# A decoder trunk on one Trainium2 core: token-major router logits, a larger ring of expert weights, whole rows to DRAM

## The chip, the core and the metric

The kernel runs on one NeuronCore of a Trainium2 chip. Its five engines run their own instruction streams in order: TensorE (PE; its weight loads are listed as PEld), VectorE (DVE), ScalarE (ACT), GpSimd (POOL) and SyncE (SP), which here only issues DMAs. What orders one engine after another are semaphores. The metric is the device time of one execution in microseconds, as the median of some runs.

## The reference, cut to what matters

Two layers, each a mixer, a cross-attention into 256 memory tokens and a mixture of experts; 256 tokens of width 1024, 16 experts of width 512.

```python
for layer in range(DEPTH):                         # DEPTH = 2
    xn = rms_norm(h, norm_mix[layer])
    h = h + (even_mixer(xn, ...) if layer % 2 == 0 else short_conv_mixer(xn, ...))
    h = h + memory_cross_attn(rms_norm(h, norm_xattn[layer]), mem, norm_mem[layer], ...)
    h = h + hier_moe(rms_norm(h, norm_ffn[layer]), ...)
return rms_norm(h, norm_final)

def hier_moe(xn, w_group, b_group, w_expert, b_expert, w_gate, w_up, w_down):
    g_prob = softmax(xt @ w_group + b_group)       # 4 groups
    g_top, g_idx = top_k(g_prob, 1)
    e_logits = (xt @ w_expert + b_expert).reshape(n, 4, 4)
    e_top, e_idx = top_k(e_logits[arange(n), g_idx[:, 0]], 2)
    w = softmax(e_top) * g_top
    ...
    for e in range(16):
        y = y + gate[:, e:e+1] * ((silu(xt @ w_gate[e]) * (xt @ w_up[e])) @ w_down[e])
```

## The kernel before

Tokens lie in two tiles of 128 (`tt` 0 and 1); the residual `h` stays in SBUF as [128, 2, 1024] in float32. A norm sums squares (`square_sum`, on ScalarE with "S", on VectorE with "V"; the squares themselves go to scratch tiles `junkS`, `junkV`), takes a power on GpSimd (`rstd_of`, L237), scales into `xs`, and TensorE transposes it through PSUM banks `nB`, `nC` (`norm_T`, L255). Projections of the mixers and of cross-attention run in split precision: each weight chunk `w` is cast on ScalarE to `hi` (L282), VectorE subtracts for `lo` (L283), both from a pool `spl` of three buffers a tag, and TensorE multiplies the token halves `xh`, `xl` with them (L324, L327, L329 into `FA`; L303 to L305 into `TA`). Layer 1 also norms and transposes the memory tokens (`mem`, halves `m1h`, `m1l`) at the start of its mixer.

The expert stage (`moe`) begins with the route. TensorE transposes `h` (L801) into banks of the tags B and C (two buffers each), copies make `hTr` (L802). The router then multiplies with its 20 columns `wr` as the stationary side and 256 tokens as the moving side (`lg`, L464), copies the result out (`lgT`, L467 and L468), turns it token-major with a small matmul against `two_id` (`lp`, L472), and VectorE adds the bias and ranks the experts (`lo` L483, `scratch` L488 to L491). The functions `busy` put filler matmuls between (L88). Meanwhile the normed tokens `xs` are made in half precision as a high part (L808, L809) and a low part: `low_part` does tile 0 on VectorE (L812), and tile 1 as a scaling on ScalarE (L816) and a subtraction on GpSimd (L817). `dispatch` builds a selection matrix `Pm` (L568) and gathers the 64 tokens of each expert by matmuls (`gB`, L101), scaled into `XgT` (L590, L592).

Experts go in eight pairs. Their weights come as 98 chunks a layer, most of 1 MB, in a fixed order (gate of pair n, down of pair n-1, up of pair n), each into a slot of `ring`; SyncE (L672) issues the next chunk of a slot once the matmuls that used its last content are done, and keeps at most eight loads under way. The ring takes buffers that are idle in that stage: `extra` (NX of 1 MB), `act8`, `kvp`, the six `w` and the three `hi`/`lo` pairs, so that with NX = 6 it has 20 slots. The results of the first six pairs go back by rows: `y` is scaled from PSUM (L743 on VectorE, L745 on ScalarE), an indirect DMA of GpSimd (L746) writes it to DRAM (`Yd`) in halves of 512 columns, and `get_rows` reads it back at the end; the last two pairs come back through a matmul (`PT`). An `If` handles experts with more than 64 tokens.

What sets the order: the framework's scheduler orders each engine's instructions by the program's dependences; `first()` raises the priority of a block, and `mm` or `keep_in_program_order` pins an instruction to the written order.

## Time and profile before

| | |
|---|---|
| median of 3 runs | 955.02 us (953.09 to 956.59) |
| profiled execution | 953.4 us, span 951.4 us |
| mean granted TensorE clock | 0.978 |
| TensorE busy | 890.1 us, 94% |
| VectorE, ScalarE, GpSimd busy | 396.8, 323.4, 82.1 us |
| moved by DMA | 285.45 MB, 300 GB/s over the span |

An execution's own time is the span from the first to the last instruction and what lies around it, here 2.0 us. A busy share is an average over stages of different kinds, so the views below are read by stage: layer 0's mixer and cross-attention up to about 266 us, its route to 285, its experts to about 500, and the same again for layer 1 with the route at 711 to 729 and the experts to about 933.

### The profile page before, as it was taken

The page shows a single profiled execution, that of the slowest core. Times are in us where ns is not written, and L with a number is a line of the kernel's source. Part 1 is how long each engine was busy: PE and PEld are TensorE (multiplying, and loading weights), DVE is VectorE, ACT ScalarE, POOL GpSimd, SP SyncE. Part 2 cuts the span into 40 slices and gives each one's busy share as a digit, 9 for nine tenths or more (in the row PEclk, how much of TensorE's full clock was granted, in tenths as well). Part 3 has the DMA queues.
Part 4 walks back from the last instruction along what each step waited for, and adds up shares of the span by engine and source line. Part 5 has one row for each costly group of instructions (what it writes and reads, how often), then busy time and mean ns, then how long its engine had stood idle before and what let it go on. Part 6 is the DMA issues. An engine that isn't in the chain of part 4 may idle for free. (4 is left out here: it accounts for less than half of the span.)

```text
span 951.4 us, 13242 instructions
## 1 busy us (share of the span) xinstructions
PE 890.1 (94%) x5205; PEld 582.5 (61%) x5205; DVE 396.8 (42%) x842; ACT 323.4 (34%) x597; POOL 82.1 (9%) x136
## 2 busy tenths in 40 slices
PE   7999999999989998899789999999998999899975
PEld 5898779898853333533238998998874333343322
DVE  5846587644452111112057655644444111112106
ACT  4545584654421111011018444635432111111002
POOL 1000060000030001000100000000003000000201
PEclk9989999999999999899999999999999999999998
DMA  7856156657969999999996556558886999999993
GB/s 255 289 185 141 28 172 206 190 202 297 364 226 404 418 420 419 415 421 418 412 385 208 183 182 199 151 174 301 319 315 244 422 417 421 415 420 418 415 407 126
DMA packets 83024, 285.45 MB, mean 300 GB/s; under 512 B 15113, under 2 KB 16225, under 8 KB 62469
## 3 DMA queue, kind: packets, MB, share of 16 engines
q1 hardware_dynamic: 78468, 272.82, 76.3%
q0 software_dynamic: 4480, 11.65, 3.3%
q8 instruction: 45, 0.74, 0.3%
q14 instruction: 31, 0.25, 0.1%
HBM read 275.94 MB, written 11.53 MB: 302 GB/s over the span
## 5 line engine op out<-in xcount | busy, mean ns | idle before, releaser
L283 DVE TENSOR_TENSOR lo<-w,hi 128x1024 fp32r<-128x1024 f32 x122 | 147.7, 1222 | 124.2 <-ACT hi L282 84.3
L282 ACT CAST hi<-w 128x1024 fp32r<-128x1024 f32 x122 | 125.9, 1046 | 87.7 <-PE FA L329 48.0
L101 PE MATMUL egA<-we,XgT 128*64 128x512 f32 x512 | 122.3, 613 | 10.4 <-DVEq L825 6.4
L101 PE MATMUL euA<-we,XgT 128*64 128x512 f32 x512 | 116.8, 593 | 6.3 <-DMA we<-in_moe_w_up_dram 6.3
L101 PEld LDWEIGHTS euA<-we,XgT 128*64 128x64 f32 x512 | 40.0, 137 | 79.1 <-issue 62.0
L101 PE MATMUL eyA<-we,hT 128*64 128x512 f32 x256 | 74.5, 609 | 9.7 <-DMA we<-in_moe_w_down_dram 6.7
L101 PEld LDWEIGHTS egA<-we,XgT 128*64 128x64 f32 x512 | 37.8, 140 | 72.7 <-issue 58.4
L101 PE MATMUL eyO<-we,hT 128*64 128x512 f32 x256 | 73.7, 607 | 0.0
L327 PE MATMUL FA<-xh,hi 128*128 128x256 f32 x272 | 70.4, 292 | 1.8 <-ACT xh L258 1.6
L329 PE MATMUL FA<-xl,hi 128*128 128x256 f32 x272 | 69.6, 289 | 1.8 <-DVE xl L259 1.8
L590 ACT ACTIVATE XgT<-gB,ffn 128x128 f32<-128x128 f32 x64 | 21.8, 365 | 132.9 <-DVE XgT L592 132.9
L327 PEld LDWEIGHTS FA<-xh,hi 128*128 128x128 f32 x272 | 53.3, 196 | 3.6 <-ACT xh L258 2.3
L329 PEld LDWEIGHTS FA<-xl,hi 128*128 128x128 f32 x272 | 53.1, 195 | 3.2 <-DVE xl L259 2.6
L101 PEld LDWEIGHTS eyA<-we,hT 128*64 128x64 f32 x256 | 20.2, 140 | 48.9 <-issue 34.7
L746 POOL DMA_INDIRECT yd<-y,row x24 | 23.9, 994 | 292.7 <-ACT y L745 273.9
L726 DVE SCALAR_TENSOR_TENSOR hs<-hs,euA 128x512 f32<-128x512 f32 x16 | 11.0, 687 | 84.2 <-PE euA L101 84.2
L101 PEld LDWEIGHTS eyO<-we,hT 128*64 128x64 f32 x256 | 20.8, 140 | 37.5 <-issue 35.8
L324 PE MATMUL FA<-xh,lo 128*128 128x256 f32 x272 | 41.7, 285 | 0.0
L101 PEld LDWEIGHTS <-xs 128*128 128x128 f16 x512 | 33.0, 146 | 13.6 <-issue 13.6
L724 ACT ACTIVATE hs<-egA 128x512 f32<-128x512 f32 x16 | 9.6, 597 | 90.8 <-PE egA L101 68.6
L237 POOL TENSOR_TENSOR rs<-ms,mhalf 128x2 f32<-128x2 f32 x9 | 6.5, 718 | 366.2 <-DVE ms L235 244.9
L743 DVE TENSOR_SCALAR y<-eyO,gslr 128x512 f32<-128x512 f32 x12 | 9.0, 751 | 69.4 <-PE eyO L101 69.4
(415 smaller groups left out, 1569.5 us busy)
## 6 DMA issues: line engine op xcount, KB each, us to landing
we<-in_moe_w_gate_dram SPq DMA_DIRECT2D x58, 1024.0 KB, 13.9
we<-in_moe_w_down_dram SPq DMA_DIRECT2D x54, 1024.0 KB, 15.5
we<-in_moe_w_up_dram SPq DMA_DIRECT2D x52, 1024.0 KB, 18.0
we<-in_moe_w_up_dram SPq DMA_DIRECT2D x24, 512.0 KB, 11.5
w<-in_odd_w_in_dram SPq DMA_DIRECT2D x12, 1024.0 KB, 11.3
w<-in_even_w_in_dram SPq DMA_DIRECT2D x9, 1024.0 KB, 9.0
w<-in_xa_wk_dram SPq DMA_DIRECT2D x8, 1024.0 KB, 5.8
w<-in_xa_wv_dram SPq DMA_DIRECT2D x8, 1024.0 KB, 5.7
```

What stands on the lines that cost most here:

```text
L101: tc.keep_in_program_order(P.matmul(out, w, src, **how))
L237: G.tensor_tensor(rs, ms, mhalf, op=ALU.pow)
L282: S.copy(hi, t)
L283: V.tensor_sub(lo, t, hi.bitcast(F32))
L324: P.matmul(o, lo[:, fs], xh[:, k, :], start=False, stop=(k == J - 1), skip_group_check=True)
L327: P.matmul(o, hi[:, fs], xh[:, k, :], start=(k == 0 and f % 2 == 0), stop=False, skip_group_check=True)
L329: P.matmul(o, hi[:, fs], xl[:, k, :], start=False, stop=False, skip_group_check=True)
L590: S.activation(Xg[pi][:, j, :], src, AF.Copy, scale=g)
L724: S.activation(hs, acc["g"], AF.Tanh, scale=0.5)
L726: V.scalar_tensor_tensor(hs, hs, 0.5, acc["u"], op0=ALU.mult, op1=ALU.mult)
L743: V.tensor_scalar(y, py[nh], gsl, None, op0=ALU.mult)
L746: G.indirect_dma_start(out=Yd[l][nh], out_offset=bass.IndirectOffsetOnAxis(ap=PT[:, 0:1], axis=0), in_=y, in_offset=None, bounds_check=2 * ...
```

## The change

Six edits. (1) The router takes `hTr` as the stationary side, 128 tokens at a time, and `wr` as the moving side of 20 columns: 16 small matmuls straight into token-major logits `lp`, with no `lgT` and no second product. `lp` holds one bank of tag C throughout. (2) The norm's factor is made per token tile; the low part of tile 0 is pinned before the factor of tile 1, the low part of tile 1 is one instruction of VectorE, pinned behind `Pm`, and the gather's matmuls with it come last. GpSimd's two subtractions go. (3) NX = 7, so the ring has 21 slots. (4) Rows go to DRAM as 1024 columns by one indirect DMA a pair, and come back so. (5) `wr` moves into the expert stage's pool, loaded ahead of it; SyncE now loads the bias `rb` of layer 0 before x. (6) The scratch tiles of the squares share the tags `hi`/`lo` with the splits, or are the PSUM bank that was just added; several small tiles share tags.

```diff
-NX = 6
+NX = 7
...
-    def load_router(l):
-        t = const.tile([128, J, 20], F32, name=f"wr{l}")
+    def load_router(l, mp):
+        t = mp.tile([128, J, 20], F32, name=f"wr{l}", tag="s2", bufs=3)
...
-    def square_sum(src, acc, eng):
-        junk = (sm if eng == "S" else mix).tile([128, 512], BF16, name="junk" + eng, tag="junk" + eng, bufs=1)
+    def square_sum(src, acc, eng, junk=None):
+        if junk is None:
+            junk = spl.tile([128, 512], BF16, name="junk" + eng, tag="hi" if eng == "S" else "lo")
...
-            square_sum(hs, ss[:, half, tt:tt + 1], "S")
+            square_sum(hs, ss[:, half, tt:tt + 1], "S", ps)
...
-        lg_ps = bank("C", "lg")[:, 0:T]
-        lgT = mp.tile([128, T], F32, name="lgT", tag="s2", bufs=3)
-        G.memset(lgT, 0.0)
-        for j in range(0, J, 2):
-            for i in (0, 1):
-                P.matmul(lg_ps[i * 64:i * 64 + 20, :], wr[l][:, j + i, :], hT[j // 4][:, j % 4 + i, :],
-                         start=(j == 0), stop=(j == J - 2))
-        busy(ident, hT[1][:, 3, :], 4)
-        V.tensor_copy(lgT[0:20, :], lg_ps[0:20, :])
-        V.tensor_copy(lgT[64:84, :], lg_ps[64:84, :])
-        between()
-        lp = bank("C", "lp")[:, 0:2 * 20].rearrange("p (t e) -> p t e", t=TT)
-        for tt in range(TT):
-            P.matmul(lp[:, tt, :], lgT[:, tt * 128:(tt + 1) * 128], two_id, start=True, stop=True)
...
+            order = [(tt, part) for tt in range(TT) for part in range(2)]
+            steps = [(j0, order) for j0 in banks]
+            if late:
+                late()
+                steps = [(j0, order[:-1]) for j0 in banks] + [(j0, order[-1:]) for j0 in banks]
...
-            y = mp.tile([128, 512], F32, name="y", bufs=2)
...
-            G.indirect_dma_start(out=Yd[l][nh], out_offset=bass.IndirectOffsetOnAxis(ap=PT[:, 0:1], axis=0), in_=y,
+            if nh == 0:
+                rows_.append(mp.tile([128, D], F32, name="y", bufs=1))
+                S.activation(rows_[0][:, 0:512], py[nh], AF.Copy, scale=gsl)
+                return
+            V.tensor_scalar(rows_[0][:, 512:D], py[nh], gsl, None, op0=ALU.mult)
+            G.indirect_dma_start(out=Yd[l], out_offset=bass.IndirectOffsetOnAxis(ap=PT[:, 0:1], axis=0), in_=rows_[0],
...
+                for tt in range(TT):
+                    rstd_of(ss_of_h[-1], tt, rs)
+                    if tt:
+                        tc.keep_in_program_order(
+                            V.scalar_tensor_tensor(xsl[:, 0, :], h[:, 0, :], rsx[:, 0:1], xsh[:, 0, :],
+                                                   op0=ALU.mult, op1=ALU.subtract))
+                    V.tensor_scalar(rsx[:, tt:tt + 1], rs[:, tt:tt + 1], SCALE, None, op0=ALU.mult)
...
+                lp = bank("C", "lp")[:, 0:2 * 20].rearrange("p (t e) -> p t e", t=TT)
...
+                            P.matmul(lp[:, tt, :], hj[:, jj, tt * 128:(tt + 1) * 128], wr[l][:, j, :],
+                                     start=(j == 0 and tt == 0), stop=(j == J - 1), skip_group_check=True)
+                busy(ident, hT[1][:, 3, :], 6)
...
-                    for c in (slice(0, 512), slice(512, D)):
-                        t = mp.tile([128, 512], F32, name="xt", tag="XgT", bufs=2)
-                        S.activation(t, h[:, 1, c], AF.Copy, scale=rsx[:, 1:2])
-                        G.tensor_sub(xsl[:, 1, c], t, xsh[:, 1, c])
+                    tc.keep_in_program_order(
+                        V.scalar_tensor_tensor(xsl[:, 1, :], h[:, 1, :], rsx[:, 1:2], xsh[:, 1, :],
+                                               op0=ALU.mult, op1=ALU.subtract))
```

Where the scheduler puts this is seen in three places. First TensorE in layer 0's route, from the last transposes of `h` to the fillers behind the logits; before:

```order
L801 MATMUL nB<-ident,h 128x128 x3
L801 MATMUL nC<-ident,h 128x128 x3
L801 MATMUL nB<-ident,h 128x128 x3
L801 MATMUL nC<-ident,h 128x128 x3
L464 MATMUL lgC<-hTr,wr_1874 20x256 x8
L88 MATMUL busyO<-hTr,ident 128x256 x4
L472 MATMUL lpC<-two_id,lgT 128x20 x2
L88 MATMUL busyO<-lgT,ident 128x256 x6
```

and now:

```order
L809 MATMUL nB<-ident,h 128x128 x6
L815 MATMUL lpC<-wr_2564,hTr 128x20 x4
L809 MATMUL nC<-ident,h 128x128 x4
L815 MATMUL lpC<-wr_2564,hTr 128x20 x8
L809 MATMUL nC<-ident,h 128x128 x4
L815 MATMUL lpC<-wr_2564,hTr 128x20 x4
L88 MATMUL busyO<-hTr,ident 128x256 x6
```

The transposes no longer run through: those of bank C come one bank after the other, with the router's matmuls on the copies between them.

Second the start of layer 1's mixer. ScalarE from the scaling of the tokens on, before:

```order
L247 ACTIVATE xs<-h,rs 128x1024
L207 ACTIVATE junkS,ss<-mem_5949 128x512
L282 CAST hi<-w 128x1024
L258 ACTIVATE xh<-nB,mix_5879 128x256
L258 ACTIVATE xh<-nC,mix_5879 128x256
```

and now, down to the first cast of `w`:

```order
L249 ACTIVATE xs<-h,rs 128x1024
L207 ACTIVATE junkS,ss<-mem_5855 128x512
L260 ACTIVATE xh<-nB,mix_5793 128x256
L260 ACTIVATE xh<-nC,mix_5793 128x256
L260 ACTIVATE xh<-nB,mix_5793 128x256 x2
L260 ACTIVATE xh<-nC,mix_5793 128x256 x2
L260 ACTIVATE xh<-nB,mix_5793 128x256
L207 ACTIVATE junkS,ss<-mem_5855 128x512 x2
L260 ACTIVATE xh<-nC,mix_5793 128x256
L207 ACTIVATE junkS,ss<-mem_5855 128x512
L284 CAST hi<-w 128x1024
```

The cast stood behind the second square of `mem` and ahead of the first `xh`; it stands behind all of both. On TensorE at the same place, now (before, 40 projection matmuls `FA` stood between the last transpose of `xs` and the sixteen of `mem`):

```order
L88 MATMUL busyO<-h,ident 128x256 x2
L329 MATMUL FA<-xh,hi 128x256
L257 MATMUL nB<-ident,mem_5855 128x128
L257 MATMUL nC<-ident,mem_5855 128x128
L257 MATMUL nB<-ident,mem_5855 128x128 x4
L257 MATMUL nC<-ident,mem_5855 128x128 x3
L257 MATMUL nB<-ident,mem_5855 128x128 x3
L257 MATMUL nC<-ident,mem_5855 128x128 x4
L331 MATMUL FA<-xl,hi 128x256
```

One projection matmul is left ahead of the memory's transposes.

Third SyncE at layer 0's restart. The loads `we` up to 2634 (before) and 2618 (now) fill the ring for the first time; the later ones wait for expert matmuls. Before:

```order
L672 DMA we_2610<-in_moe_w_gate_dram 128x2048
L672 DMA we_2624<-in_moe_w_up_dram 128x1024
L672 DMA we_2626<-in_moe_w_up_dram 128x1024
L672 DMA we_2628<-in_moe_w_up_dram 128x1024
L672 DMA we_2630<-in_moe_w_up_dram 128x1024
L672 DMA we_2632<-in_moe_w_up_dram 128x1024
L672 DMA we_2634<-in_moe_w_up_dram 128x1024
L672 DMA we_2829<-in_moe_w_gate_dram 128x2048
L672 DMA we_2831<-in_moe_w_gate_dram 128x2048
```

and now:

```order
L659 DMA we_2594<-in_moe_w_gate_dram 128x2048
L659 DMA we_2606<-in_moe_w_up_dram 128x2048
L659 DMA we_2608<-in_moe_w_up_dram 128x1024
L659 DMA we_2610<-in_moe_w_up_dram 128x1024
L659 DMA we_2612<-in_moe_w_up_dram 128x1024
L659 DMA we_2614<-in_moe_w_up_dram 128x1024
L659 DMA we_2616<-in_moe_w_gate_dram 128x1024
L659 DMA we_2809<-in_moe_w_gate_dram 128x2048
L659 DMA we_2811<-in_moe_w_gate_dram 128x2048
L659 DMA we_2618<-in_moe_w_gate_dram 128x1024
```

The last half chunk of the first filling, 2618, stands behind two loads (2809, 2811) that wait for expert matmuls. In layer 1 the whole ring is filled ahead of the first such load.

## Rows read from the trace of the kernel before

**Rows 1.** Busy by stretch: PE, PEld, DVE, ACT, POOL busy, clock, DMA share, GB/s
```profile
280.00:285.00 5.00, 5.00 (x40) 2.38 (x39) 1.35 (x5) 1.36 (x4) 2.22 (x9) 1.00 0.02 5
520.00:530.00 10.00, 10.00 (x85) 10.00 (x85) 5.50 (x5) 3.83 (x6) 0.00 (x0) 1.00 0.63 210
900.00:910.00 10.00, 7.37 (x24) 1.99 (x21) 0.00 (x0) 0.00 (x0) 0.00 (x0) 0.83 1.02 412
```
**Rows 2.** SyncE's timeline (start, us, issues): the restart in layer 0 and layer 1
```profile
284.80 0.80 SPq L672 DMA_DIRECT2D we<-in_moe_w_gate_dram  x2
...
728.85 4.53 SPq L672 DMA_DIRECT2D we<-in_moe_w_gate_dram  x4
```
**Rows 3.** DMA view from 300 to 360 us, in layer 0's expert stage
```profile
DMA packets 4110, 25.16 MB, mean 419 GB/s; under 512 B 575, under 2 KB 575, under 8 KB 1507
```
**Rows 4.** Timeline of TensorE in layer 0's route (start, us, operation, count, idle before)
```profile
267.38 0.60 PE L801 MATMUL nB<-ident,h 128*128 128x128 f32 x3 [0.78 <-DVE h L223]
...
269.04 1.91 PE L464 MATMUL lgC<-hTr,wr 128*20 128x256 f32 x16
...
273.46 0.59 PE L472 MATMUL lpC<-two_id,lgT 128*128 128x20 f32 x4 [0.58 <-DVE lgT L468]
...
278.95 2.24 PE L101 MATMUL gB<-Pm,xs 128*128 128x128 f16 x32 [1.08 <-DVE Pm L568]
281.12 3.65 PE L101 MATMUL egA<-we,XgT 128*64 128x512 f32 x16
```
**Rows 5.** The same of VectorE
```profile
270.48 0.75 DVE L808 TENSOR_SCALAR xs<-h,rsx 128x1024 f16<-128x1024 f32 x1
271.27 1.28 DVE L812 SCALAR_TENSOR_TENSOR xs<-h,rsx,xs 128x1024 f16<-128x1024 f32 x1
...
274.09 0.38 DVE L483 SCALAR_TENSOR_TENSOR lo<-lpC,rs,rb 128x20 f32<-128x20 f32 x2 [0.78 <-PE lpC L472]
274.51 1.23 DVE L488 TENSOR_TENSOR scratch<-lo 128x160 f32<-128x160 f32 x1
275.66 0.31 DVE L490 TENSOR_TENSOR scratch<-lo 128x160 f32<-128x160 f32 x1
...
278.60 0.51 DVE L568 TENSOR_TENSOR Pm<-iota,posm 128x128 f16<-128x128 f32 x2
```
**Rows 6.** The same of ScalarE
```profile
268.36 1.25 ACT L802 COPY hTr<-nC 128x512 f32<-128x512 f32 x2 [0.22 <-PE nC L801]
```
**Rows 7.** The same of GpSimd
```profile
274.40 1.16 POOL L817 TENSOR_TENSOR xs<-xt,xs 128x512 f16<-128x512 f32 x1 [0.83 <-ACT xt L816]
```
**Rows 8.** Timeline of TensorE at the start of layer 1's mixer
```profile
505.35 0.58 PE L327 MATMUL FA<-xh,hi 128*128 128x256 f32 x2
...
511.86 0.67 PE L255 MATMUL nB<-ident,mem 128*128 128x128 f32 x4
...
513.63 0.36 PE L327 MATMUL FA<-xh,hi 128*128 128x256 f32 x1
```
**Rows 9.** The same of ScalarE
```profile
503.65 1.03 ACT L282 CAST hi<-w 128x1024 fp32r<-128x1024 f32 x1
...
507.70 0.66 ACT L207 ACTIVATE junkS<-mem 128x512 bf16<-128x512 f32 x1
...
508.31 1.07 ACT L282 CAST hi<-w 128x1024 fp32r<-128x1024 f32 x1
509.25 0.51 ACT L258 ACTIVATE xh<-nC,mix 128x256 fp32r<-128x256 f32 x1
509.88 1.15 ACT L247 ACTIVATE mem<-mem,rs 128x1024 f32<-128x1024 f32 x1
```
**Rows 10.** Busy by stretch at the program's start, columns as in rows 1
```profile
12.40:13.90 1.50, 0.38 (x1) 0.19 (x1) 1.50 (x3) 0.98 (x4) 0.00 (x0) 1.00 0.63 95
16.00:18.40 2.40, 2.40 (x14) 2.23 (x13) 0.96 (x6) 1.47 (x2) 0.00 (x0) 0.50 1.05 404
```
**Rows 11.** SyncE's timeline at the program's start
```profile
1.63 0.42 SPq L168 DMA_DIRECT2D mix<-in_norm_mix_dram  x1
```

More of the change, by code (lines that the diff above doesn't have):

```diff
@@ L152, in hybrid_trunk_kernel @@
     dram = ctx.enter_context(tc.tile_pool(name="rows_of", bufs=1, space=bass.MemoryType.DRAM))
-    Yd = [[dram.tile([2 * T, 512], F32, name=f"yd{l}{nh}") for nh in range(2)] for l in range(2)]
+    Yd = [dram.tile([2 * T, D], F32, name=f"yd{l}") for l in range(2)]
     def clear_rows():
-        z = mix.tile([128, 512], F32, name="zero", tag="Pu", bufs=2)
+        z = mix.tile([128, D], F32, name="zero", tag="Pu", bufs=2)
         G.memset(z, 0.0)
         for l in range(2):
-            for nh in range(2):
-                for c in range(4):
-                    nc.gpsimd.dma_start(Yd[l][nh][c * 128:(c + 1) * 128, :], z)
+            for c in range(4):
+                nc.gpsimd.dma_start(Yd[l][c * 128:(c + 1) * 128, :], z)
     gains = {}
@@ L230, in new_ss, with rstd_of @@
         return ss
[L232 removed]
+    def rstd_of(ss, tt=None, rs=None):
         ms = sm.tile([128, TT], F32, name="ms")
[L234 to L237 removed]
+        if rs is None:
+            rs = sm.tile([128, TT], F32, name="rs")
+        c = slice(0, TT) if tt is None else slice(tt, tt + 1)
+        V.tensor_add(ms[:, c], ss[:, 0, c], ss[:, 1, c])
+        V.tensor_scalar(ms[:, c], ms[:, c], 1.0 / D, EPS, op0=ALU.mult, op1=ALU.add)
+        G.tensor_tensor(rs[:, c], ms[:, c], mhalf[:, c], op=ALU.pow)
         return rs
@@ L537, in route @@
         G.tensor_mul(wb, wa, m2)
-        first_w = small("first_w", NG, 4)
+        first_w = small("second", NG, 4)
         G.tensor_mul(first_w, one, wa[:, :, None].to_broadcast([128, NG, 4]))
@@ L570, in dispatch @@
         N = n * CAP
-        Xg = [mp.tile([128, J, 128], F32, name="XgT", tag=x_tag, bufs=2 if x_tag == "XgT" else 1) for _ in range(n // 2)]
+        Xg = [mp.tile([128, J, 128], F32, name="XgT", tag=x_tag) for _ in range(n // 2)]
         per = 512 // N
         def gather(lo, hi):
-            banks = {}
-            for j0 in range(lo, hi, per):
-                ps = bank("B", "g").rearrange("p (j s) -> p j s", j=per)
-                for jj in range(per):
-                    i = 0
-                    for tt in range(TT):
-                        for part in xs:
-                            mm(ps[:, jj, :], part[:, tt, :, j0 + jj], Pm[:, tt].rearrange("p e s -> p (e s)"),
-                               start=(i == 0), stop=(i == 3))
-                            i += 1
-                banks[j0] = ps
+            banks = {j0: bank("B", "g").rearrange("p (j s) -> p j s", j=per) for j0 in range(lo, hi, per)}
+            order = [(tt, part) for tt in range(TT) for part in range(2)]
[3 more added lines that the diff above has]
+                steps = [(j0, order[:-1]) for j0 in banks] + [(j0, order[-1:]) for j0 in banks]
+            for j0, parts in steps:
+                for jj in range(per):
+                    for tt, part in parts:
+                        mm(banks[j0][:, jj, :], xs[part][:, tt, :, j0 + jj], Pm[:, tt].rearrange("p e s -> p (e s)"),
+                           start=(jj == 0 and (tt, part) == order[0]), stop=((tt, part) == order[-1]),
+                           skip_group_check=True)
             for pi in range(n // 2):
@@ L789, in moe @@
             mp = mctx.enter_context(tc.tile_pool(name=f"moe{l}", bufs=1, reuse_waits="tile"))
+            with first():
+                load_router(l, mp)
             if fill is not None:
@@ L847, in experts @@
                     with first() if n == 0 else nullcontext():
-                        (pair,), last_part = dispatch(mp, l, xs, vals, posm, 2 * n, 2, n < ROWS_PAIRS)
+                        (pair,), last_part = dispatch(mp, l, xs, vals, posm, 2 * n, 2, n < ROWS_PAIRS,
+                                                      late=None if n else low_part)
                     if n == BREAK:
```

51 lines of the change are left out of this document (20 added, 31 removed).

## The prediction

> **What bounds the kernel now.** I read the busy shares by stretch first. TensorE is full in the mixer and cross-attention stretches (10.00 of 10 us at 520 to 530), while in the late expert stretch it is busy 7.37 of 10 and the DMA engines are full [rows 1]. So each layer is two problems in series: a matmul stretch, whose end is moved by anything that stops TensorE, and a stream of expert weights at 419 GB/s [rows 3], whose end is its restart plus the bytes still to come. The link is the route. By then the ring is full, the DMA engines do nothing (share 0.02 at 280 to 285), and SyncE issues again only when the first expert matmuls have released a slot, at 284.80 in layer 0 and 728.85 in layer 1 [rows 1, 2]. Hence three questions: does TensorE reach the route sooner, is the route shorter, and how many bytes are in the ring by then? The profiled execution took 953.4 us (span 951.4); the median of the runs is 955.0. I sum changes against the execution and add the sum to the median.
>
> **Start, term 0.** The bias rows of the router are now issued ahead of x. A small load costs SyncE 0.42 us [rows 11], two about 0.85, and x is waited for at once. Against that, the first scaled tile leaves ScalarE after one weight cast instead of two, about a microsecond sooner [a cast: rows 9]. I take 0, range -2 to +1, since TensorE is short of work here and its clock had already fallen (0.50 at 16.00 to 18.40 after 0.38 busy of 1.50 us at 12.40) [rows 10]: a smoother start could avoid that.
>
> **Route, term +0.2 in layer 0.** Before: transposes from 267.38, eight wide router matmuls, copies, two small matmuls, and the logits are used at 274.09 [rows 4, 5]. The new form has sixteen float32 matmuls of 20 columns. Each is two records. The 20-column records go by at about 0.11 us (four in 0.59, the last lasting some 0.26), the 256-column ones at 0.12 (sixteen in 1.91) [rows 4]: the narrow moving side saves nothing, so a matmul costs 0.22 and sixteen 3.5, against 1.91 + 0.59. Also the logits occupy one of the two C banks, so the order is a chain: two transposes (0.5), copy (0.65, half of 1.25 [rows 6]), four matmuls (0.9), four transposes (0.6), copy (0.65), eight matmuls (1.8), four transposes (0.6), copy (0.65), four matmuls (0.9): 7.2, with hand-offs 7.5, so 274.8 or +0.7. In return, GpSimd's two subtractions go. The first ranking step takes 1.23 us while the second subtraction runs (274.40 to 275.56), and its neighbour of the same shape takes 0.31 [rows 5, 7]: -0.9, and the same pair stands once more in layer 1. Last, the low part of tile 1 now follows both selection matrices: 278.60 + 0.51 + 1.28 = 280.4, then the last 8 of 32 gather matmuls (0.6), 281.0, against 281.12 for the first expert matmul [rows 4, 5]. But the scalings between the two have no longer started meanwhile: +0.4. Sum +0.2. Bounds: -3.0, if the small matmuls cost next to nothing, and +1.5, if every hand-off costs what the waits before these rows show (0.58 to 1.08 [rows 4]).
>
> The Trainium skill ("TensorE: Matmul & The Clock Gate", section "Wait — 56ns, not 53.3ns?") puts the floor between matmul starts at about 25 ns however few the columns. Thirty-two records would then cost 0.8 us, an estimate from that page, and not 3.5. The 20-column records of this trace are more than four times that apart.
>
> **Layer 1's route, term +0.6.** The same +0.2, and here the 0.75 us high part of tile 0 stands on VectorE ahead of the last h add, of which about half was idle waiting before: 0.4, an estimate [rows 5]. Range -2.6 to +2.
>
> **The extra slot.** In layer 1 a whole 1.05 MB chunk more is in before the restart, with the same idle DMA engines to take it as the window of layer 0 shows: 1.05/419 = -2.5 us. In layer 0 SyncE's order puts the second half of the new chunk behind two chunks that wait for the first expert matmuls (the third order shown with the change), so only half counts: -1.25. Both ranges reach to 0 and, for layer 0, to -2.5. Here the cover matters: the loads of the slot run while the DMA engines are idle.
>
> **Whole rows, term -0.4.** The bytes are the same, GpSimd's issues are off the path, and fewer, longer packets in a full stream can give a little back. Range -1 to 0.5.
>
> **Start of layer 1's mixer, term +5.2: the largest.** The scratch of the squares now rotates with the `hi` splits, and the scheduler has put the first cast of w last. Before: cast at 503.65, seven scalings, two squares, cast at 508.31; the first projection matmul at 505.35; then 40 of them before the sixteen memory transposes at 511.86, which end at 513.63 [rows 8, 9]. Now the first cast gives way to one more scaling and one more square: 508.31 - 1.03 + 0.51 + 0.66 = 508.45, so TensorE's first projection matmul is at 509.5, not 505.35. The second of its row order is already a memory transpose, which waits for the scaling of mem. That came 2.2 after the last square [rows 9], now 507.8 + 2.2 = 510.0, ends 1.15 later at 511.15, and the transposes take 1.77: TensorE is past them at 512.9 with 1 projection matmul done. Before it was past them at 513.63 with 40. At 0.118 a matmul (85 in 10 us [rows 1]) that is 39 x 0.118 - 0.7 = +3.9. TensorE is full from there to the route, so nothing gives it back. I add 1.2: at the start of the program less idle time came before 2.40 us at half clock [rows 10], and TensorE would be idle here for some 4 of 6 us; half of that stretch is 1.2. Bounds: 0 (the casts keep ahead and TensorE makes it up) to +6.5 (two such stretches, or splits on VectorE that arrive late).
>
> The Trainium skill (same page, section "What's actually happening") says that the default state is throttled and activity releases it; the row at the start agrees, and without that term the sum would be 1.2 lower.
>
> **Sum.** 0 + 0.2 + 0.6 - 1.25 - 2.5 - 0.4 + 5.2 = +1.85: 955.25 on the execution, 956.9 on the median. A measurement of this kernel can tell 0.3%, or 2.9 us, from no change: 952.2 to 957.9 is the same.
>
> **Rivals.**
> A, forecast: the mixer start's debt eats what the slots give. 956.9; chance 0.42.
> B, slower: the router chain. Each transposed pair needs a bank, the bank needs a copy, the copy an engine that has normed tokens in its queue. If each of the six hand-offs costs 0.25 more than I gave, each route is 1.5 longer; it decides where the logits are used later than 276. 956.9 + 3.0 = 959.9; chance 0.25. For: waits of 0.58 to 1.08 stand between these very steps [rows 4]. Against: ScalarE's two copies followed each other without a gap [rows 6].
> C, slower: the end of the stream. With 21 slots the last lap reuses only the last 14 (98 modulo 21) instead of 18; a chunk waits for the one 14 before it, and 8 loads are in flight. It decides if TensorE lags six chunks behind. One chunk late in each layer is 2 x 2.5: 961.9; chance 0.07. Against: TensorE waits for DMA there (7.37 of 10 [rows 1]).
> D, faster: the debt of the mixer start is absorbed. Without 5.2: 951.7; chance 0.16. For: the last rows of an in-order queue can overtake nothing, but 40 matmuls are short. Against: 10.00 of 10.
> E, faster: the small matmuls stream instead of waiting for their stationary loads. 3.0 less in each route: 950.9; chance 0.10. Against: the 0.11 of rows 4. By the skill's floor of 25 ns, quoted above, it would be this one.
>
> **The numbers.** Predicted 956.9. Faster D + E, 0.26; same A, 0.42; slower B + C, 0.32. The range leaves out about one in ten at either end: low where D gains the route's bound as well, 949.0; high where B meets the mixer start's upper bound (956.9 + 3.0 + 1.3 = 961.2), 961.5.
>
> **What would show it.** In the profile after: the first projection matmul of layer 1's mixer some 4 us after the last token transpose, its memory transposes directly behind it, and a granted clock under 1.00 there; the ranking step at about 0.3 us; the logits used 7.2 to 7.5 us after the transposes begin; SyncE's restart 0.2 later than now relative to the last h add, with half a chunk (layer 0) and a chunk (layer 1) more issued before it. I am wrong if TensorE has done tens of projection matmuls by the memory transposes, if the router matmuls' records stand closer than 0.1 us, or if the stream's last lap shows SyncE waiting for TensorE.

## The result, and the profile of the changed kernel

The changed kernel takes 964.91 us (median of seven runs, 961.87 to 969.45), the kernel before 955.02 us: a ratio of 1.0103, 95 % interval 1.0064 to 1.0141. The prediction was 956.9 us with a range up to 961.5, so the change costs 9.9 us where 1.9 were forecast, and the time lies outside the range.

The table cuts the profiled executions at marks that each trace has: the transposes of the memory rows (nA), the last addition to h ahead of each router, the first expert matmul (egA), the last down projection (eyA), and the scaling of layer 1's normed tokens (xs). All in us; the last columns are experiments, told below.

| stretch | before | after | e1 old route | e2 mixer | e10 fillers | c4 |
|---|---|---|---|---|---|---|
| start to nA | 38.12 | 37.52 | 37.58 | 37.54 | 37.48 | 37.48 |
| nA to last h add, layer 0 | 228.51 | 231.31 | 224.04 | 223.57 | 227.85 | 223.76 |
| route, layer 0 | 14.49 | 20.18 | 13.33 | 20.20 | 15.16 | 13.84 |
| egA to last eyA, layer 0 | 206.91 | 205.27 | 205.31 | 205.65 | 203.87 | 205.81 |
| last eyA to xs | 13.95 | 16.63 | 15.34 | 16.57 | 13.69 | 16.28 |
| xs to last h add, layer 1 | 208.72 | 214.22 | 213.23 | 208.41 | 214.25 | 208.00 |
| route, layer 1 | 14.47 | 18.66 | 13.34 | 20.18 | 15.18 | 13.86 |
| egA to last eyA, layer 1 | 206.48 | 203.99 | 204.33 | 204.10 | 204.19 | 203.88 |
| to the end | 19.75 | 19.72 | 19.70 | 21.38 | 19.73 | 21.39 |
| span | 951.4 | 967.5 | 946.2 | 957.6 | 951.4 | 944.3 |

The kernel before was timed again beside each group of experiments, at 955.9 to 957.1 us. Each ratio below is to the median beside it, so a plain difference from 964.9 carries some 2 us of that.

The profiled execution of the changed kernel, 969.45 us, is the slowest of its seven: its span is 16.1 us longer, the medians differ by 9.9. Two rows of the table hold 5.5 us that one trace of each kernel can't lay to the change: nA to the last h add (+2.80) and last eyA to xs (+2.68). Kernels with the same instructions there take 222.9 to 231.3 us and 13.7 to 16.6 us in the traces of this case, and what differs is the granted clock; from 490 to 500 us of the changed kernel it was 0.67. For the second row this is less sure (see what stays open). Without these two, 10.6 us are left, near the 9.9 of the medians: both routes (+5.69, +4.19), the mixer's start (+5.50), the two streams (-1.64, -2.49), the start (-0.60).

**The routes.** Timeline of TensorE in layer 0's route of the changed kernel (start, us, operation, out<-in, count, idle before and what ended it), where [rows 4] stood:

```profile
269.57 0.94 PE L809 MATMUL nB<-ident,h 128*128 128x128 f32 x6 [0.78 <-DVE h L223]
271.00 1.36 PE L815 MATMUL lpC<-wr,hTr 128*128 128x20 f32 x8 [0.49 <-issue]
272.20 1.09 PE L809 MATMUL nC<-ident,h 128*128 128x128 f32 x4
273.97 3.60 PE L815 MATMUL lpC<-wr,hTr 128*128 128x20 f32 x16 [0.68 <-ACT hTr L811]
277.41 1.09 PE L809 MATMUL nC<-ident,h 128*128 128x128 f32 x4
279.18 1.90 PE L815 MATMUL lpC<-wr,hTr 128*128 128x20 f32 x8 [0.68 <-ACT hTr L811]
280.91 4.95 PE L88 MATMUL busyO<-hTr,ident 128*128 128x256 f32 x12
285.70 0.17 PE L494 MATMUL cntC<-selb,upper_b 128*128 128x16 bf16 x1
```

The chain is the one that was predicted: transposes, copy, products, in this order, with waits of 0.49 and 0.68 between them. But sixteen product records take 3.60 us, 0.225 each, not 0.11, and the fillers 0.41 each, so that they are still running when the counting matmuls behind them could start. The same stretch by two-microsecond windows (busy time of PE, PEld, DVE, ACT, POOL with counts, granted clock, DMA share, GB/s) says why:

```profile
265.83:268.83 3.00, 2.96 (x14) 1.93 (x12) 1.03 (x4) 0.72 (x2) 0.56 (x1) 1.00 0.05 22
268.83:270.83 2.00, 0.94 (x6) 0.75 (x6) 1.31 (x3) 0.72 (x2) 0.00 (x0) 1.00 0.68 156
270.83:272.83 2.00, 1.82 (x11) 1.86 (x12) 2.00 (x6) 0.00 (x0) 0.46 (x1) 0.68 0.98 397
272.83:274.83 2.00, 1.32 (x7) 0.92 (x6) 0.81 (x2) 0.59 (x1) 1.07 (x1) 0.50 1.02 430
278.83:280.83 2.00, 1.65 (x8) 1.65 (x8) 0.00 (x0) 1.34 (x2) 0.00 (x0) 0.50 1.02 420
```

The granted clock falls from 1.00 to 0.50, that is from 2.4 to 1.2 GHz, within the second window of the route, and stays there until the fillers behind the products. In the kernel before it is 1.00 through both routes; the first two windows of its layer 0:

```profile
266.63:268.63 2.00, 1.25 (x11) 1.25 (x12) 1.30 (x3) 1.00 (x3) 0.00 (x0) 1.00 0.72 176
268.63:270.63 2.00, 1.94 (x20) 1.04 (x18) 1.15 (x6) 1.05 (x3) 0.71 (x1) 1.00 0.85 350
```

VectorE shows the consequence, and that the collision of [rows 5] is gone:

```profile
281.12 0.38 DVE L468 SCALAR_TENSOR_TENSOR lo<-lpC,rs,rb 128x20 f32<-128x20 f32 x2 [7.03 <-PE lpC L815]
281.54 0.33 DVE L473 TENSOR_TENSOR scratch<-lo 128x160 f32<-128x160 f32 x1
286.01 0.19 DVE L500 SCALAR_TENSOR_TENSOR posm<-cntC,selb 128x32 f32<-128x32 f32 x1 [1.41 <-PE cntC L498]
```

The logits are used 11.55 us after the transposes begin (281.12 - 269.57), where 7.2 to 7.5 had been worked out; the ranking step takes 0.33 instead of 1.23; and VectorE then waits 1.41 for counts that stand behind the slow fillers. SyncE's restart moves by the whole of it: its first load that waits for an expert matmul is issued 23.86 us after the last addition to h (292.69), 18.17 in the kernel before (284.80), where 0.2 later was predicted.

**The mixer's start** in layer 1, ScalarE and TensorE of the changed kernel, against [rows 8, 9]:

```profile
515.88 0.67 ACT L207 ACTIVATE junkS<-mem 128x512 bf16<-128x512 f32 x1
516.49 0.51 ACT L260 ACTIVATE xh<-nC,mix 128x256 fp32r<-128x256 f32 x1
516.85 0.67 ACT L207 ACTIVATE junkS<-mem 128x512 bf16<-128x512 f32 x1
517.46 1.08 ACT L284 CAST hi<-w 128x1024 fp32r<-128x1024 f32 x1
518.86 1.15 ACT L249 ACTIVATE mem<-mem,rs 128x1024 f32<-128x1024 f32 x1 [0.32 <-POOL rs L239]
518.59 0.58 PE L329 MATMUL FA<-xh,hi 128*128 128x256 f32 x1 [3.90 <-ACT hi L284]
519.75 0.45 PE L257 MATMUL nB<-ident,mem 128*128 128x128 f32 x1 [0.58 <-DVE mem L248]
523.06 0.56 PE L331 MATMUL FA<-xl,hi 128*128 128x256 f32 x1
```

The first projection matmul waits 3.90 us for the cast, the memory transposes come directly behind it at half clock, and TensorE is past them 12.15 us after the scaling of xs (523.06 - 510.91) with one projection matmul done, as predicted (10.9 and 1.2 for the clock).

### The profile page after: what moved, and what is told of

The parts are those of the page before. It is cut to its first block, busy times and chain, and to the rows that moved or that the text cites. A ratio compares the mean times of both kernels' runs of the same rounds, so it can differ in the third digit from the quotient of the medians.

```text
span 967.5 us, 13204 instructions
## 1 busy us (share of the span) xinstructions
PE 904.2 (93%) x5213; PEld 592.2 (61%) x5213; DVE 396.0 (41%) x846; ACT 321.0 (33%) x593; POOL 60.5 (6%) x104
## 5 line engine op out<-in xcount | busy, mean ns | idle before, releaser
L101 PE MATMUL eyA<-we,hT 128*64 128x512 f32 x256 | 72.5, 620 | 5.9 <-ACT hT L720 3.0
L331 PE MATMUL FA<-xl,hi 128*128 128x256 f32 x272 | 71.7, 295 | 1.1 <-DVE xl L261 1.0
L101 PE MATMUL eyO<-we,hT 128*64 128x512 f32 x256 | 69.0, 593 | 0.0
L326 PEld LDWEIGHTS FA<-xh,lo 128*128 128x128 f32 x272 | 36.9, 194 | 0.2
L101 PE MATMUL gB<-Pm,xs 128*128 128x128 f16 x512 | 35.1, 226 | 1.2 <-DVE Pm L553 1.2
## 6 DMA issues: line engine op xcount, KB each, us to landing
we<-in_moe_w_up_dram SPq DMA_DIRECT2D x56, 1024.0 KB, 16.1
```

The lines of the kernel that those rows point to most:

```text
L101: tc.keep_in_program_order(P.matmul(out, w, src, **how))
L326: P.matmul(o, lo[:, fs], xh[:, k, :], start=False, stop=(k == J - 1), skip_group_check=True)
L331: P.matmul(o, hi[:, fs], xl[:, k, :], start=False, stop=False, skip_group_check=True)
```

## The experiments

Theory 1: the loss is the route (its clock) and the mixer's order. Its main rivals: the route's hand-offs and the bank that the logits hold; the narrow products as such; and that the stream takes up whatever the earlier stages lose. All experiments start from the changed kernel.

### e1_old_route: the old router inside the changed kernel

```diff
-                            P.matmul(lp[:, tt, :], hj[:, jj, tt * 128:(tt + 1) * 128], wr[l][:, j, :], ...
+                        P.matmul(lg_ps[i * 64:i * 64 + 20, :], wr[l][:, j + i, :], hT[j // 4][:, j % 4 + i, :], ...
...
+                    P.matmul(lp[:, tt, :], lgT[:, tt * 128:(tt + 1) * 128], two_id, start=True, stop=True)
```

> Both layers' router products as in the kernel before (the twenty columns of weights held, h streamed, a copy of the logits, the product with two_id); the rest of the changed kernel kept, the later low parts and the 21st slot too. Theory 1 (the loss sits in the new router chain, which is 5.7 us longer in layer 0 and 4.2 us longer in layer 1 in the changed kernel's trace): from the last addition to h to the first egA back to about 14.5 us in both layers, granted clock 1.00 there, and the time about 10 us under the changed kernel's 964.9, at 955. Theory 2 (the route's delay is absorbed by the stream, and the loss is the mixer's order and the start): the route short again, but the time within 3 us of 964.9. If the old router beside the later low part is short too, at 13.6 us, the low part's move is worth the 0.9 us of the collision by itself.

Measured: 954.51 us, ratio to before 0.9974 (0.9940 to 1.0007), 10.4 us under the changed kernel. Both routes take 13.3 us at a granted clock of 1.00 throughout; the windows that answer to those above:

```profile
261.62:263.62 2.00, 1.26 (x11) 1.26 (x12) 1.31 (x3) 1.01 (x3) 0.00 (x0) 1.00 0.68 160
263.62:265.62 2.00, 1.94 (x14) 0.84 (x12) 2.00 (x6) 0.89 (x2) 0.46 (x1) 1.00 0.97 393
```

So the new router holds the larger part of the loss, and the stream doesn't take it up. Beside the old router the later low parts and the gone subtractions are worth 1.2 us in each layer (14.49 to 13.33), a little more than the collision.

### e2_mixer_start and e12_squares_apart: the start of layer 1's mixer

e12 has only the second piece of this diff, e2 both:

```diff
-        S.copy(hi, t)
+        with first() if boost else nullcontext():
+            S.copy(hi, t)
...
-            junk = spl.tile([128, 512], BF16, name="junk" + eng, tag="hi" if eng == "S" else "lo")
+            junk = (extra_[0].tile([128, 512], BF16, name="junk" + eng, tag="x") if extra_ else
+                    spl.tile([128, 512], BF16, name="junk" + eng, tag="hi" if eng == "S" else "lo"))
```

> Only the discarded outputs of the squares change place (in layer 1 they go to a slot of the tag x instead of the tags hi and lo), and the first rounding of weights of layer 1's mixer is put ahead of the normed tokens' copies. Theory: with the squares of the memory rows out of the way of the first cast, that cast ends before the transposes of the normed tokens are copied, the wait of 3.90 us before the first FA goes, and the mixer starts as in the kernel before or up to 2 us earlier; the time about 5.5 us under the changed kernel, at 959.5 (959 to 962). Rival: the mixer's earlier start is taken up by the wait for weights later in layer 1, as in the prediction's case of a debt absorbed: then last addition to h of layer 1 does not move by more than 2 us and the time stays at 963 to 965.

> One half of e2_mixer_start alone: the discarded squares go to a slot of the tag x in layer 1; the first rounding of weights is left where the scheduler puts it. In the program the four squares of the memory rows then stand ahead of the squares of h, but the first cast stands behind seven scalings of the normed tokens (2.5 us). Theory (the order on ScalarE is what costs: the first cast decides when the mixer begins, and how many squares stand ahead of it): from the scaling of the normed tokens to the last addition to h of layer 1, 209.5 to 211.5 us, between the 208.2 of e2_mixer_start and the 214.2 of the changed kernel; time 961 to 963. Rival (the shared buffers themselves cost, as waits of the casts for a buffer): 208.4, as e2_mixer_start, and 959.5 to 961.5.

Measured: e2 961.53 us, ratio to before 1.0066 (1.0039 to 1.0092); e12 959.69 us, 1.0045 (1.0012 to 1.0077). From xs to the last h add of layer 1: 208.41 and 208.65 us against 214.22. The whole predicted term is there. It is not absorbed either: the experts behind it take as long as in the changed kernel (204.10 and 204.15 against 203.99). The medians alone, 3.4 and 5.2 us lower, could not show that. e12 misses its expectation (209.5 to 211.5), and the rival named in it (208.4) came out. TensorE and ScalarE of e12:

```profile
506.10 0.45 ACT L261 ACTIVATE xh<-nB,mix 128x256 fp32r<-128x256 f32 x1
508.59 1.08 ACT L285 CAST hi<-w 128x1024 fp32r<-128x1024 f32 x1
508.39 0.69 PE L258 MATMUL nB<-ident,mem 128*128 128x128 f32 x4 [0.61 <-DVE xl L262]
509.92 0.36 PE L330 MATMUL FA<-xh,hi 128*128 128x256 f32 x1
```

The cast still ends late, at 509.67, and the first projection matmul is 2.5 us later than in e2, yet nothing is lost: with their squares out of the way the memory rows are scaled early, and three of the four groups of memory transposes, work that TensorE has to do anyway, fill its wait. So it was the squares' sharing of the casts' buffers, which put them between the normed tokens and the cast, that cost 5.5 us; the place of the cast alone costs 0.2 in these two traces.

### e4_wide_router: 64 columns

```diff
-        t = mp.tile([128, J, 20], F32, name=f"wr{l}", tag="s2", bufs=3)
+        t = mp.tile([128, J, 64], F32, name=f"wr{l}", tag="s2", bufs=3)
+        G.memset(t, 0.0)
```

> The router's streaming side is padded from 20 to 64 columns with zeros; everything else as in the changed kernel. Theory A (the clock falls because of the narrow products: granted clock 0.72 over the route in the changed kernel): with three times the columns the granted clock over the route stays nearer 1.00, the 32-record group falls from 3.60 us to about 2, and the route of 20.2 us gets 2 to 4 us shorter, the time 4 to 7 us. Theory B (the chain of transposes, copies and products is long by itself, hand-off after hand-off, and its gaps take the clock down): the products get no shorter, the route stays at 20 us or more and the time within 2 us of 964.9.

Measured: 961.64 us, ratio 1.0048 (1.0018 to 1.0078). The two layers run the same program and came out differently: 15.07 us in layer 0, 20.17 in layer 1. The middle products of each, and the window over them:

```profile
271.51 2.00 PE L816 MATMUL lpC<-wr,hTr 128*128 128x64 f32 x16 [0.68 <-ACT hTr L812]
719.64 3.68 PE L816 MATMUL lpC<-wr,hTr 128*128 128x64 f32 x16 [0.68 <-ACT hTr L812]
271.10:273.10 2.00, 1.59 (x14) 1.59 (x15) 0.81 (x2) 1.06 (x2) 1.07 (x1) 1.00 0.98 414
720.73:722.73 2.00, 2.00 (x12) 2.00 (x11) 0.00 (x0) 0.00 (x0) 0.00 (x0) 0.50 0.88 320
```

This is the cleanest pair of the study: one program, one execution, and 5.1 us between the route at full clock and the one that lost it. At full clock layer 0's route costs 0.6 us more than before, where +0.2 was predicted. Neither theory had one layer gain 5.1 us and the other none. Width alone doesn't hold the clock: layer 1 lost it with the same 64 columns.

### e5_lp_other_bank: both C banks for the transposes

```diff
-                lp = bank("C", "lp")[:, 0:2 * 20].rearrange("p (t e) -> p t e", t=TT)
+                lp = bank("O", "lp")[:, 0:2 * 20].rearrange("p (t e) -> p t e", t=TT)
...
-                busy(ident, hT[1][:, 3, :], 6)
+                busy(ident, hT[1][:, 3, :], 6, "A")
```

> The logits are gathered in the PSUM bank O instead of C, so that both banks of tag C serve the transposes, and the six fillers behind the route write to a bank of tag A. Theory B1 (the loss in the route is that the logits hold one of the C banks from the first product on, so that the second pair of transposes through C waits for the products of the first): the chain from the first transpose to the last product of the logits falls from 11.55 us by 2 to 3 us and so does each layer's route, the time by 4 to 6 us. Theory A (half clock and hand-offs set the chain): under 1 us per layer, time within 2 us of 964.9.

Measured: 964.17 us in five runs (955.0 to 965.35), ratio 1.0064 (1.0013 to 1.0115): the time tells nothing apart. The routes take 14.42 and 17.11 us, so the chain does get shorter, while the clock still falls in both:

```profile
268.85 2.16 PE L815 MATMUL lpO<-wr,hTr 128*128 128x20 f32 x16
718.53 3.44 PE L815 MATMUL lpO<-wr,hTr 128*128 128x20 f32 x16
```

The held bank is a real cost: at full clock the route is 1.3 us shorter without it (15.16 in e10, 13.84 in c4, both below). It does not explain the clock. With both banks the transposes run through again, and TensorE is as busy at the start of this route as in the kernel before; the clock falls all the same, only later (and in layer 0 for a shorter time). Layer 1:

```profile
712.55:714.55 2.00, 1.25 (x11) 1.26 (x11) 1.30 (x3) 1.00 (x3) 0.00 (x0) 1.00 0.95 354
714.55:716.55 2.00, 2.00 (x20) 1.89 (x18) 2.00 (x6) 0.30 (x1) 0.46 (x1) 1.00 1.02 403
716.55:718.55 2.00, 1.33 (x5) 0.95 (x6) 0.81 (x2) 1.29 (x2) 1.07 (x1) 0.71 0.94 272
```

### e8_wide240 and e9_fillers: more columns, or work inside the chain

e8, the twenty columns streamed twelve times:

```diff
-                            P.matmul(lp[:, tt, :], hj[:, jj, tt * 128:(tt + 1) * 128], wr[l][:, j, :],
+                            P.matmul(lpw[:, tt, :].rearrange("p (r e) -> p r e", r=12), hj[:, jj, tt * 128:(tt + 1) * 128],
+                                     wr[l][:, None, j, :].to_broadcast([128, 12, 20]),
```

e9, three fillers at each later step of the chain:

```diff
+                    if jp2:
+                        busy(ident, hT[(jp2 - 1) // 2][:, (jp2 - 1) % 2 * 2 + 1, :], 3)
```

> In the new router each product streams the twenty weight columns twelve times over (240 columns, of which the first twenty are used); instructions, order and banks are those of the changed kernel. Theory A (the narrow products take the clock down): the granted clock stays 1.00 through both routes, the route is 15.1 us as in layer 0 of the 64-column run, not 20.2 us, and the time 8 to 10 us under the changed kernel's 964.9, at 955 to 957. Theory B (the idle time between transposes, copies and products takes it down, whatever is streamed): at least one route in two falls to 0.50 again and lasts 20 us or, since the wider products stream at half clock, up to 24 us; time 962 to 969.

> The changed kernel with three fillers of 256 columns at each of the three later steps of the router chain, in the stretches where TensorE waits for a copy; products of twenty columns as in the changed kernel. At full clock the nine fillers (0.24 us each) lengthen the chain by 0.7 to 1.5 us. Theory B (idle time takes the clock down): granted clock 1.00 through the routes, 16 to 16.6 us each, time 957 to 959. Theory A (narrow products): half clock in most routes still, each then 21 us or more, time 964 to 969.

Measured: e8 961.15 us, ratio 1.0047 (1.0014 to 1.0081), routes 18.07 and 19.61; e9 963.79 us, 1.0065 (1.0027 to 1.0104), routes 18.73 and 18.72. Neither theory's numbers came out. e8 was badly sized: at full clock its sixteen records take 3.51 us against 2.00 for 64 columns, so its 18.07 is a route at full clock with products of nearly twice the length. e9 was badly sized too: three of its fillers take 1.46 us at full clock, two records each, so nine cost about 4 and not 2.2. But the windows of layer 1 in e8 (first three lines) and layer 0 in e9 (the others) tell more than the times:

```profile
721.34:723.34 2.00, 1.84 (x6) 1.66 (x7) 1.98 (x5) 0.00 (x0) 1.14 (x1) 0.69 0.96 383
723.34:725.34 2.00, 1.99 (x7) 1.29 (x6) 0.15 (x1) 1.15 (x1) 0.39 (x1) 0.50 0.91 266
725.34:727.34 2.00, 1.34 (x7) 1.26 (x8) 0.00 (x0) 0.59 (x1) 0.00 (x0) 0.96 0.97 342
267.42:269.42 2.00, 1.82 (x13) 1.85 (x14) 2.00 (x6) 0.06 (x1) 0.46 (x1) 0.86 0.91 377
269.42:271.42 2.00, 2.00 (x6) 1.55 (x6) 0.81 (x2) 1.24 (x2) 1.07 (x1) 0.50 1.02 430
273.42:275.42 2.00, 2.00 (x17) 1.90 (x16) 0.00 (x0) 0.00 (x0) 0.00 (x0) 1.00 1.01 395
```

In these three routes (layer 1 of e8, both of e9) the clock falls at about the same place as in the changed kernel, which points at the waiting at the start of the route. But it then comes back within the chain, where the changed kernel with narrow products and waits stays at 0.50. And in layer 0 of e8, with the same waits at the start, it does not fall at all:

```profile
268.81:270.81 2.00, 0.94 (x6) 0.75 (x6) 1.30 (x3) 0.72 (x2) 0.00 (x0) 1.00 0.68 156
270.81:272.81 2.00, 1.83 (x10) 1.76 (x11) 2.00 (x6) 0.00 (x0) 0.46 (x1) 1.00 0.92 381
```

### e10_start_fillers: work in the waits at the start

```diff
             stream = Stream(chunks_ahead(l), ring)
+            busy(ident, h[:, 0, 512:768], 8)
             with first():
```

> The changed kernel with eight fillers of 256 columns that go where TensorE has nothing to do at the start of the router: two to four before the transposes of h, two before the first products, two before the second; products of twenty columns as in the changed kernel. In the runs so far the clock falls about 4 us into the route even where the first products are 240 columns wide, so what stands ahead of it is the waiting at the start. Theory C (the waiting at the start takes the clock down, the narrow products only keep it down): granted clock 1.00 through both routes, 15.1 to 15.6 us each, time 8 to 9 us under the changed kernel's 964.9, at 955.5 to 957. Theory A (narrow products take it down by themselves): it falls all the same, a little later, and the routes stay at 18 to 20 us, the time at 962 to 966.

Measured: 956.96 us, ratio 0.9987 (0.9943 to 1.0031), 8.0 us under the changed kernel. The routes take 15.16 and 15.18 us with the same narrow products and the same bank:

```profile
265.12 1.03 PE L88 MATMUL busyO<-h,ident 128*128 128x256 f32 x4
266.07 0.94 PE L810 MATMUL nB<-ident,h 128*128 128x128 f32 x6
266.85 1.03 PE L88 MATMUL busyO<-h,ident 128*128 128x256 f32 x4
269.89 1.93 PE L816 MATMUL lpC<-wr,hTr 128*128 128x20 f32 x16
265.33:267.33 2.00, 2.00 (x13) 1.59 (x12) 1.30 (x3) 0.72 (x2) 0.00 (x0) 1.00 0.75 168
267.33:269.33 2.00, 2.00 (x17) 1.92 (x16) 2.00 (x6) 0.10 (x1) 0.46 (x1) 1.00 0.91 377
```

Eight throw-away matmuls that take next to no time of their own, since TensorE was waiting there (15.16 us, 15.07 without them in layer 0 of e4), give back 8.5 us in the two routes of the traces (5.02 and 3.48).

Theory C's forecast came out, and what is shown is the remedy: with the waits filled the clock holds over twenty columns. That the first waits alone take it down is not shown. With twenty columns and no fillers at the start it fell in twelve routes of twelve (two each of the changed kernel, e2, e5, e7, e9, e12), with 64 or 240 columns in two of four (e4, e8); and e5 lost it with no more waiting at its start than the kernel before has. So the width of the products seems to have a part in it too.

### e7_nx6: 20 slots again

```diff
-NX = 7
+NX = 6
```

> The changed kernel with 20 slots for weights instead of 21, nothing else. Theory (the 21st slot shortens each restart as the prediction's slot terms say; in the traces so far the stretch from the first egA to the last euA of layer 1 is 197.5 us in the kernel before and 195.0 to 195.6 in all those with 21 slots): that stretch goes back to 197 to 197.5 in layer 1 and to 197.5 to 198 in layer 0, and the time is 3 to 4 us over the changed kernel's 964.9, at 968 to 969. Rival (the whole rows, not the slot, shorten the stretch): it stays at 195 and 196.2, the time at 964 to 966.

Measured: 967.42 us in four runs, ratio 1.0113 (1.0040 to 1.0185); the time can't be told from the changed kernel's. The trace tells more. From the first egA to the start of the last up projection (euA), the mark of the expectation, layer 1 takes 197.57 us, where the twelve traces with 21 slots have 194.7 to 196.4; layer 0 takes 197.46, where they have 194.4 to 197.9. So in layer 1 the slot is worth 1.2 us or more, 2.6 against the changed kernel; in layer 0 these traces can't tell it from nothing. The whole rows are worth next to nothing: with them and 20 slots, first egA to last eyA is 206.51 and 206.84 us, 0.4 shorter than before in layer 0 and 0.4 longer in layer 1.

### c1_old_route_mixer, c2_new_route_held, c4_held_narrow: the parts put together

c1 is e1 with e2's mixer. c2 is the new router with e5's bank, e10's fillers, products of 120 columns, and e2's mixer; c4 is c2 with twenty columns. The edits of c4's route:

```diff
-            busy(ident, hT[1][:, 3, :], 6)
+            busy(ident, hT[1][:, 3, :], 6, "A")
...
+            busy(ident, h[:, 0, 512:768], 8, "A")
...
-                lp = bank("C", "lp")[:, 0:2 * 20].rearrange("p (t e) -> p t e", t=TT)
+                lp = bank("O", "lp")[:, 0:2 * 20].rearrange("p (t e) -> p t e", t=TT)
```

> The old router and the mixer's start put right together (the edits of e1_old_route and e2_mixer_start), with the 21st slot, the whole rows and the later low parts of the change. If the two costs add, the 2.2 us that e1_old_route stands under the kernel before and the 5.5 us of the mixer's start make 949 (947.5 to 951.5), 0.8 % under the kernel before. If the stream takes the mixer's gain up, it stays at 953 to 955.

> The new router with what the runs so far say it lacks: logits in bank O so that both banks of tag C serve the transposes, products of 120 columns (the twenty streamed six times, a length that a transposed column block already has), the start fillers, and the mixer's start of e2_mixer_start. If the clock holds, each route is 12.5 to 13.5 us, as short as the old router beside the later low parts (13.3 us), and the time 949 to 951, level with the old router's combination (950.6). If the clock falls in it, the routes are 14.5 to 17 us and the time 953 to 958.

> c2_new_route_held with products of twenty columns again: logits in bank O, the start fillers, the mixer's start. Theory C (filling the waits is what holds the clock; the width of the products does not matter once they are filled): granted clock 1.00 in both routes, 14.3 to 14.6 us each as in c2_new_route_held, and its time, 947 to 950. Theory A+C (both are needed): the clock falls in at least one of the two routes, 16 to 18 us there, and the time is 950 to 953.

Measured: c1 950.64 us, ratio 0.9924 (0.9893 to 0.9956); c2 947.75 us, 0.9908 (0.9875 to 0.9942); c4 947.18 us, 0.9922 (0.9892 to 0.9952). All three beat both kernels; the intervals can't rank them. At a clock of 1.00 throughout, the routes are c1 13.32 and 13.33 us, c2 14.54 and 14.56, c4 13.84 and 13.86. c4's windows in layer 0:

```profile
261.24:263.24 2.00, 2.00 (x15) 1.63 (x13) 1.30 (x3) 0.99 (x3) 0.00 (x0) 1.00 0.67 156
263.24:265.24 2.00, 2.00 (x20) 1.91 (x19) 2.00 (x6) 0.32 (x1) 0.45 (x1) 1.00 0.94 389
265.24:267.24 2.00, 2.00 (x17) 1.90 (x16) 0.81 (x2) 1.29 (x2) 1.07 (x1) 1.00 1.04 438
```

c4 is e5 with the waits filled (and the mixer's start), and it keeps the clock that e5 lost. With the waits filled, twenty columns do better than 120: c2's products stand so that the last transposes come 1.0 us later (266.09 against 265.20, from last h adds at 261.17 and 261.24). And the new router, even held at full clock, is no shorter than the old one beside the later low parts. By these traces, what pays in this change is the slot, the low parts' place and the gone subtractions.

## Why the prediction was wrong, step by step

**The routes (+0.2 and +0.6 predicted; +5.7 and +4.2 in the profiled execution, +5.7 in each layer of e2 and e12).** This is the step that failed, and by its bounds too (+1.5 and +2). The work in it was counted about right: at full clock the same chain takes 15.07 (e4, 64 columns) and 15.16 us (e10), +0.6 to +0.7, and the logits are used 8.0 to 8.1 us after the transposes begin, against 7.2 to 7.5. The other 8.5 us of the two routes are the clock's. What the prediction left out is the clock: it priced all of these rows at that of the kernel before. It had such a case in hand: it put 1.2 us of half clock on the mixer's start because TensorE would wait there. It did not ask the same of the route, although its own chain, with one bank and a copy between every two steps, is a list of waits. The two-microsecond windows of the kernel before (shown above) had the sign: TensorE is busy only 1.25 of 2.00 us right after the last h add even there, where the clock still held.

**Rival B** named the right place and the right mark (logits used later than 276: they were used at 281.12, or 278.9 counted from the last addition to h as before), but its mechanism was hand-offs at 0.25 each, and its 3.0 us were a third of the loss. The prediction's own steps hold 5.3 us of matmuls in the chain (0.5, 0.9, 0.6, 1.8, 0.6, 0.9); at the half clock of [rows 10] they double, and about 5 us for each route would have come out.

**The mixer's start (+5.2, though its parts add up to 5.1; measured +5.5).** Right in size, and right in its working: the first projection matmul 7.68 us after the scaling of xs (7.5 worked out), memory transposes directly behind it, and half clock over them. Rival D, that the debt is absorbed, is refuted by e2 and e12. The reason given, the place of the cast, is only half the truth: e12 shows that a late cast costs 0.2 us if the memory rows are early.

**The slots (-1.25 and -2.5; measured -1.6 and -2.5 with the rows).** The sizes came out; e7 bears out that of layer 1, and in layer 0 the spread of the traces hides it. The whole rows (-0.4) gave nothing that e7 can tell.

**The start (0; measured -0.6 at nA).** Within its range; the other traces with the change lie between -0.7 and +0.4 of the one before, so it can't be told from 0.

**The collision (-0.9)** came as predicted (1.23 to 0.33), and with the old router it can be seen as a gain (e1).

**Rival C**, the end of the stream, is not seen: ahead of its last two groups of up-projection matmuls TensorE waits for DMA in the changed kernel as before, 1.35 and 1.33 us in layer 0 and 2.61 and 0.17 in layer 1, against 2.19 and 1.47, 1.31 and 1.32. **Rival E** is refuted: at full clock sixteen records of twenty columns take 1.93 us (e10), 0.12 each. By the Trainium skill ("TensorE: Matmul & The Clock Gate", section "Wait — 56ns, not 53.3ns?"), which the prediction quoted, starts never come closer than about 25 ns. The float32 records stay far above that; the five counting matmuls of the route, in bfloat16 and 16 columns wide, reach it (0.025 us apart, from 285.70 to 285.80 in the changed kernel).

The sum by the measured terms: -0.6 + 5.7 + 4.2 - 1.6 - 2.5 + 5.5 = 10.7, against 9.9 between the medians. The prediction's sum was 1.85. The two routes alone stand 9.1 us above their terms, the other terms together a little under theirs. The two rows of the table that were set aside (+5.5) are in neither sum.

**What stays open.** Sixteen routes have the new products and no fillers at the start; the clock held in two of them, layer 0 of e4 and of e8, both with wider products. Why in these and not in layer 1 of the same executions was not settled, nor which it needs, the waits, the narrow products or both. Nor was the fall under the last down projection of layer 0 (last eyA to xs: 13.7 us at full clock, up to 16.6), which comes in nine of the traces with the change and not in e5, e7, e8, e10 or the kernel before. With one trace of the kernel before, that this fall comes with the change is neither shown nor excluded.

## What to carry to other kernels

Where an edit turns one long run of matmuls into a chain of short ones with a copy between each two, price the chain at half of TensorE's clock as well as at full, and ask what keeps the engine occupied in its waits. Throw-away matmuls in the waits of the chain cost some 0.1 us here and held the clock in all six routes where they stood from its start on. And a buffer that is lent out is an edge in the order: discarded outputs that share the buffers of a cast stood ahead of that cast here.

## What the runs showed of the hardware that was not expected

The clock fell with no long idle time ahead: in layer 0 of the changed kernel the waits are 0.78 and 0.49 us, TensorE is busy 0.94 and 1.82 of 2.00 us in the two windows, and the clock is down within the second. The Trainium skill ("TensorE: Matmul & The Clock Gate", section "HAM oscillation — how this bites in real kernels") describes the same fall behind waits for DMA that are each longer than the bursts of matmuls between them; here each wait is shorter than the work behind it (0.78 us before 0.94 of transposes, 0.49 before 1.36 of products), and it came in fourteen of the sixteen routes with the new products and no fillers at the start.

It also did not come back while TensorE was busy with narrow work: in the changed kernel it is 0.50 in a window with 1.65 of 2.00 us busy, but 1.00 again in e8 and e9, whose products are wide or have fillers between them. At full clock a float32 record takes 0.12 us with 20 (1.93 for sixteen) and 0.125 with 64 columns (2.00), 0.12 with 120 (2.91 for 24, c2) and 0.22 with 240 (3.51): widths up to 120 cost the same. The old router's 256-column products at 0.12 [rows 4] were read as a sign that 256 columns cost no more either; the fillers of the same width take 0.24 a record (2.84 for twelve, e10). Those products are issued in pairs to different rows of the bank, and in the trace of the kernel before the two records of a pair start some 0.02 us apart or less and the next pair 0.215 later, which is the distance from one filler's record to the next. So two went at once, and 256 columns do cost more than 20; the prediction's sum took the 1.91 us as a whole and is not touched.

That the squares now write back into PSUM added waits of TensorE (1.07 us ahead of one poB group in layer 0), but the stretch around them is no longer than before where the clock holds (13.69 us in e10, 13.95 before).
